# A down-projection whose range of row pairs moves by one per output pair, with results added to the residual in memory by DMA

## The chip, the cores and the metric

The kernel runs on one core of a Trainium2 chip. The metric is device time in microseconds: the median of several runs. A profile of one execution shows each engine: TensorE (PE, its weight loads apart as PEld), VectorE (DVE), ScalarE (ACT), GpSimd (POOL) and SyncE (SP), and the DMA queues.

## The reference, cut to what matters

One layer for 592 tokens (16 meta tokens, 512 of a prompt, 8 x 8 samples), model width 2048, all in fp32. After a mixer (recurrent and convolution heads) whose result is added to x, comes the part that the change touches:

```python
xn2 = rmsnorm(x, g_ffn)
up = jnp.einsum("btd,df->btf", xn2, w_up)          # 2048 -> 2 x 6144
gate, val = jnp.split(up, [D_FF], axis=-1)
gate_c, new_fconv = causal_dwconv(gate, st_fconv, conv_f_w)   # width 3
hid = jax.nn.gelu(gate_c + conv_f_b) * val
x = x + jnp.einsum("btf,fd->btd", hid, w_down)     # 6144 -> 2048
```

and then a final RMSNorm of x.

## The kernel before

Tokens lie along the free axis, features on the 128 partitions: 16 blocks of model rows, 48 of hidden rows. Each fp32 matmul is three fp32r ones (`hi*hi`, `hi*lo`, `lo*hi`): ACT rounds to the high part (`wh`, `fh`), DVE subtracts it for the low part (`wl`, `fl`).

The FFN (function `ffn`) multiplies pairs of blocks by halves of the tokens (290 wide in the up-projection, `H1`; 288 in the down-projection, `H2`) by the Strassen-Winograd scheme: 7 products instead of 8 (`PROD`, into four PSUM tiles, `BANKS`). For it, weights are summed on DVE (`raw`) and so are the right-hand sides (`forms`: `xt`, `fh`, `fl`, 7 forms of a row pair, which sit in one of 8 slots `h0..h7`, `l0..l7`). A *unit* is one row pair times one output pair: 7 products of 3 matmuls. A *group* of weights (`FG`, made by `ffn_groups`) is two units: SP loads 512 KB into one of two `raw` tiles, and `prep` makes `wh` and `wl`, 1792 wide, in two buffers each (`w_p`). `weights(q)` calls it one group ahead.

- Start: when the mixer ends, ACT and DVE split x1 into 16 `ph`/`pl`, POOL sums the squares and stores x1 into `xd`. Plain groups (`p`) go first; the norm stands behind the second of them. `build_x` then makes the 8 row pairs' forms in the slots.
- Up-projection: for each pair of hidden blocks a gate job (`done_f`: `combine`, `conv`, gelu) and a value job (`done_v`, which stores the hidden pair into `hd`).
- Down-projection: 22 row pairs, cut by `DSUB` into passes of 8, 8 and 6. Each pass goes through all 8 output pairs (job `("d", s, p)`). `build_h` loads a row pair from `hd` on POOL's queue and makes its forms; the next pass's are called during the last output pair of the pass before (or the last value job). `load_xp` loads the residual of an output pair, `done_d` adds the four PSUM tiles to it in seven operations on DVE, and, in the first two passes, stores it into `xe`.
- Tail (`t`): four hidden blocks that are left go through plain matmuls (`kh`, `kl`), `done_t` adds them to `xp`, and the final norm follows.

The order on each engine is set by a scheduler from the order of the code and its priorities (`urgent`, `high_priority`); a tile waits for the reader of its buffer's last use, and each engine runs its queue in order. `done_d` before:

Of the kernel before, what the change touches and what calls it, by code (L numbers as in the profile page):

```python
# [7 lines left out]
F32 = mybir.dt.float32  # L8
# [46 lines left out]
DSUB = (8, 8, 6)  # L55
NPL = 4
NTL = 4
SLOT = 8192
# [101 lines left out]
def ffn_groups():  # L160

    gs = []
    for r in range(NPL // 2):
        cols = [(0, 1), (NF, NF + 1)][r]
        for k0 in range(0, KD, 4):
            gs.append(("p", r, k0, [("w_up", k, c) for k in range(k0, k0 + 4) for c in cols]))

    def quad(src, f1, f2, kps):  # L170
        kk = [(k, c) for k, c in ((1, f2), (0, f1), (1, f1), (0, f2))]
        return [(src, 2 * kp + k, c) for k, c in kk for kp in kps]

    for m in range(NPL // 4, NF // 2):
        for o in (0, NF):
            for g in range(KD // 4):
                gs.append(("s", ("f" if o == 0 else "v", m), g, quad("w_up", o + 2 * m, o + 2 * m + 1,
                                                                 (2 * g, 2 * g + 1))))
    k0 = 0
    for s, n in enumerate(DSUB):  # L180
        for p in range(KD // 2):
            for g in range(n // 2):
# [12 lines left out]
PROD = {"P1": (0, 0), "P2": (1, 1), "R7": (2, 4), "R4": (3, 6), "Q3": (4, 2), "P6": (5, 5),  # L195
        "P5": (6, 3)}
BANKS = (("P6",), ("P2", "Q3"), ("P1", "R7"), ("P5", "R4"))
SBT = {"c": ("sb",), 0: ("sb", "o"), 1: ("sb", "z", "ev"), 2: ("sb", "z", "ev")}
X1T = ("fb", "v", "o", "z", "ev", "st", "sb", "xt")


def ffn(ctx, tc, xstack, one, dram, x1, rstd, ones, epst, warm, cv, wf, sfc, out, fst):

# [28 lines left out]
    w_p = pool("fw", 2)  # L232
# [6 lines left out]
    QP = MP - H1  # L239
# [3 lines left out]
    state = {"raw": 0, "spl": 0}  # L243

# [7 lines left out]
    def prep():  # L252
        q = state["spl"]
        while state["raw"] < min(q + 2, len(FG)):
            load()
        t = raws.pop(q)
        kind, _, i, _ = FG[q]
        if kind == "s":
            r = t.rearrange("p (s c) f -> p s (c f)", s=8)
            tt(r[:, 4:6], r[:, 2:4], r[:, 0:1].to_broadcast([P, 2, 2 * P]), AD)  # L260
            tt(r[:, 6], r[:, 5], r[:, 2], AD)
            tt(r[:, 7], r[:, 6], r[:, 1], AD)
            hi = w_p.tile([P, 7, 2 * P], F32R, tag="wh", name="wh")
            lo = w_p.tile([P, 7, 2 * P], F32R, tag="wl", name="wl")
            act(hi, r[:, 1:8], AF.Copy)
            tt(lo, r[:, 1:8], hi.bitcast(F32), SU)
        else:
            if kind == "p":
                hi = w_p.tile([P, 8, P], F32R, tag="wh", name="wh")
                lo = w_p.tile([P, 8, P], F32R, tag="wl", name="wl")  # L270
            else:
                j, o = divmod(i // 2, 2)
                if o == 0:
                    tail["h", j] = sl.tile([P, 16, P], F32R, tag=f"h{j}", name="th")
                    tail["l", j] = sl.tile([P, 16, P], F32R, tag=f"l{j}", name="tl")
                hi, lo = (tail[c, j][:, 8 * o:8 * o + 8] for c in "hl")
            act(hi, t[:, 0:8], AF.Copy)
            tt(lo, t[:, 0:8], hi.bitcast(F32), SU)
        spls[q] = (hi, lo)
        state["spl"] += 1  # L280

    tail = {}

    def weights(q, ahead=1):
        with tc.high_priority(offset=100):
            while state["spl"] <= min(q + ahead, len(FG) - 1):
                prep()
# [914 lines left out]
```

## Time and profile before

| what | us |
|---|---|
| median of 3 runs | 2752.55 (2749.21 to 2754.59) |
| the profiled execution's own time | 2755.04 |
| its span | 2753.3 |
| PE busy | 2621.3 |
| DVE busy | 1995.5 |
| ACT busy | 1127.9 |
| POOL busy | 506.4 |

All durations come from that one profiled execution, 2.5 us above the median. Its mean granted clock was 0.979 of full speed. By time, the mixer takes the span to 933 us, the up-projection goes to about 2060, the down-projection to about 2670, and the tail to the end. A stretch is read by its length against the number of matmuls that ran in it; in the waits of an engine, a row names who was waited for, how long in all, how often and how long at most. A PSUM tile is called `sgl` or `dbl`.

### The profile page before, as it was taken

What the parts mean: (1) busy time and instruction counts of PE and PEld (TensorE: products, weight loads), DVE (VectorE), ACT (ScalarE), POOL (GpSimd) and SP (SyncE); (2) the same over time, 40 slices, a digit from 0 to 9 for tenths busy, and PEclk for the clock granted to TensorE, in tenths of its full rate; (3) what the DMA queues carried; (4) which work ended last, traced back from release to release, by engine and by line L of the source; (5) the groups of instructions that cost most, each with busy time, mean ns of one, the idle gap of its engine ahead of it and who ended that gap; (6) DMA issues with size and microseconds to landing.
All of it is one profiled execution on the core that took longest, in us unless ns stands there. A gap on an engine that the chain in (4) does not pass through costs nothing. (4 is left out here: it accounts for less than half of the span.)

```text
span 2753.3 us, 45507 instructions
## 1 busy us (share of the span) xinstructions
PE 2621.3 (95%) x18974; PEld 2584.0 (94%) x18974; DVE 1995.5 (72%) x2534; ACT 1127.9 (41%) x1428; POOL 506.4 (18%) x665
## 2 busy tenths in 40 slices
PE   8999999999999989999999999999996997997987
PEld 8999999999999979999999999999996997997977
DVE  8663556546457598787878777878778779778776
ACT  5543434244234445444444444444444224223233
POOL 3341323223233511010101010101002002001002
PEclk9999999999999989999999999999998999998998
DMA  4222222222223333333333333333335444444232
GB/s 163 76 89 80 77 85 77 85 77 85 82 67 123 125 122 104 108 101 109 102 107 103 105 99 110 101 107 104 102 101 181 142 143 158 147 152 162 87 119 81
DMA packets 85406, 299.38 MB, mean 109 GB/s; under 512 B 10128, under 2 KB 14352, under 8 KB 85200
## 3 DMA queue, kind: packets, MB, share of 16 engines
q1 hardware_dynamic: 68720, 233.47, 27.5%
q0 software_dynamic: 16048, 62.55, 6.5%
q8 instruction: 149, 2.44, 0.4%
q14 instruction: 57, 0.47, 0.1%
q10 hardware_dynamic: 432, 0.46, 0.1%
HBM read 262.63 MB, written 33.80 MB: 108 GB/s over the span
## 5 line engine op out<-in xcount | busy, mean ns | idle before, releaser
L543 PE MATMUL dbl<-fh,wh 128*128 128x290 f32 (+1 forms) x3264 | 975.2, 299 | 20.6 <-DVE xp L211 15.7
L543 PE MATMUL dbl<-fl,wh 128*128 128x290 f32 (+1 forms) x3264 | 974.0, 299 | 1.3 <-DVE fl L211 1.3
L543 PE MATMUL dbl<-fh,wl 128*128 128x290 f32 (+1 forms) x3264 | 970.4, 299 | 3.0 <-DVE wl L211 3.0
L217 ACT ACTIVATE wh<-raw 128x1792 fp32r<-128x1792 f32 (+1 forms) x280 | 471.4, 1684 | 809.8 <-DVE raw L211 573.7
L211 DVE TENSOR_TENSOR wl<-raw,wh 128x1792 fp32r<-128x1792 f32 (+1 forms) x280 | 560.0, 2000 | 210.6 <-ACT wh L217 204.6
L543 PEld LDWEIGHTS dbl<-fh,wh 128*128 128x128 f32 x3264 | 623.2, 191 | 27.9 <-DVE xp L211 18.0
L543 PEld LDWEIGHTS dbl<-fh,wl 128*128 128x128 f32 x3264 | 623.5, 191 | 4.0 <-DVE wl L211 4.0
L543 PEld LDWEIGHTS dbl<-fl,wh 128*128 128x128 f32 x3264 | 623.7, 191 | 1.9 <-DVE fl L211 1.9
L211 DVE TENSOR_TENSOR raw<-raw 128x256 f32<-128x256 f32 (+1 forms) x816 | 416.0, 510 | 106.1 <-DMA raw<-wf 98.0
L1113 PE MATMUL ps<-xh,wl 128*128 128x290 f32 (+4 forms) x1536 | 336.8, 300 | 2.9 <-DVE wl L720 2.9
L1113 PE MATMUL ps<-xl,wh 128*128 128x290 f32 (+4 forms) x1536 | 335.1, 300 | 0.0
L732 ACT ACTIVATE wh<-raw 128x512 fp32r<-128x512 f32 x277 | 172.7, 628 | 395.5 <-PE ps L1113 341.1
L1113 PE MATMUL ps<-xh,wh 128*128 128x290 f32 (+4 forms) x1536 | 332.3, 298 | 2.3 <-ACT wh L732 1.7
L720 DVE TENSOR_TENSOR wl<-raw,wh 128x512 fp32r<-128x512 f32 x192 | 153.3, 804 | 193.6 <-ACT wh L732 193.3
L1113 PEld LDWEIGHTS ps<-xh,wl 128*128 128x128 f32 x1536 | 258.0, 191 | 3.1 <-DVE wl L720 3.1
L1113 PEld LDWEIGHTS ps<-xh,wh 128*128 128x128 f32 x1536 | 257.6, 191 | 3.3 <-ACT wh L732 1.9
L1113 PEld LDWEIGHTS ps<-xl,wh 128*128 128x128 f32 x1536 | 256.0, 190 | 0.0
L543 PE MATMUL sgl<-fh,wl 128*128 128x290 f32 (+1 forms) x544 | 172.7, 318 | 29.7 <-DVE wl L211 28.7
L543 PE MATMUL sgl<-fh,wh 128*128 128x290 f32 (+1 forms) x544 | 165.2, 304 | 37.7 <-ACT wh L217 34.2
L720 POOL TENSOR_TENSOR wl<-raw,wh 128x512 fp32r<-128x512 f32 x86 | 117.0, 1360 | 312.2 <-ACT wh L732 302.4
L543 PE MATMUL sgl<-fl,wh 128*128 128x290 f32 (+1 forms) x544 | 164.7, 303 | 2.9 <-DVE fl L211 2.9
L543 PEld LDWEIGHTS sgl<-fh,wl 128*128 128x128 f32 x544 | 104.7, 192 | 45.2 <-DVE wl L211 44.4
(214 smaller groups left out, 3291.0 us busy)
## 6 DMA issues: line engine op xcount, KB each, us to landing
raw<-wf SPq DMA_DIRECT2D x288, 512.0 KB, 3.6
raw<-w SPq DMA_DIRECT2D x135, 512.0 KB, 3.6
hd<-v POOLq DMA_DIRECT2D x24, 576.0 KB, 3.3
xe<-xp POOLq DMA_DIRECT2D x16, 576.0 KB, 3.8
xp<-xe POOLq DMA_DIRECT2D x16, 576.0 KB, 4.2
sb<-hd POOLq DMA_DIRECT2D x44, 144.0 KB, 2.5
sb<-hd POOLq DMA_DIRECT2D x22, 288.0 KB, 3.4
x<-x SPq DMA_DIRECT2D x16, 296.0 KB, 5.4
```

The source lines that it names most:

```text
L211: return (e or V).tensor_tensor(out=o, in0=a, in1=b, op=op)
L217: A.activation(out=o, in_=a, func=f, **k)
L543: mm = nc.tensor.matmul(o, l[a], r[z], start=i == 0 and u == 0 and k == 0, stop=i == n - 1 and u == 1 and k == 2)
L720: return (e or V).tensor_tensor(out=o, in0=a, in1=b, op=op)
L732: A.activation(out=o, in_=a, func=f, **k)
L1113: mm = nc.tensor.matmul(ps[:, b, 0:n], l, r[:, c0:c0 + n], start=(first and m == 0), stop=(last and m == 2))
```

## The change

It does five things. (1) The down-projection's passes are cut differently for each output pair (`CUT`), so that the range of row pairs moves by one from an output pair to the next: the first pass has 4, 5, 6, 7, 8, 8, 9, 9 units, the second 9 each, the third the rest (9 down to 4). There are nine slots (`NSL`), the ninth in buffers of the up-projection; `build_h` is called where `due` says: row pairs 0 to 3 in the last value job, 4 to 8 and 13 to 17 one at a time early in a job, 9 to 12 and 18 to 21 in four successive units of the last output pair of a pass. (2) `done_d` copies PSUM to tiles `e6`, `e23`, `e17`, `e54` on ACT, and five DMAs on POOL's queue add them to `xa` and `xb` in DRAM (in the first pass the two into `xb` write instead); `xa` gets the residual when the mixer ends, in 16 more stores. The tail loads `xa`, then adds `xb` into the tile by DMA. (3) Weights are split by half groups, 896 wide, in five buffers (`NWB`), prepared up to four halves ahead; their pool opens after x1's room is given back. (4) `combine`, `conv` and the hidden pair work on tiles in another layout: the convolution runs over 656 columns instead of 592, and the sample state comes by one small load per pair. (5) `kf`, `kh` and the tail's weights have rooms that come free earlier.

The diff, cut:

```diff
-DSUB = (8, 8, 6)
+CUT = [(0, a, a + 9, 22) for a in (4, 5, 6, 7, 8, 8, 9, 9)]
+NSL = 9
+NWB = 5
+TAILW = (4, 5, 0, 1)
...
-    w_p = pool("fw", 2)
...
     def prep():
-        q = state["spl"]
+        q, u = divmod(state["spl"], 2)
...
+            src, n = r[:, 1:8, u * P:u * P + P], 7
...
+            hi = w_p.tile([P, n, P], F32R, tag="wh", name="wh")
+            lo = w_p.tile([P, n, P], F32R, tag="wl", name="wl")
+            act(hi, src, AF.Copy)
+            tt(lo, src, hi.bitcast(F32), SU)
...
-    def weights(q, ahead=1):
+    def weights(q, ahead=NWB - 1):
...
-        nc.gpsimd.dma_start(out=xd[kp][:, o], in_=v)
+        nc.gpsimd.dma_start(out=xd[kp][:, 1 - o], in_=v)
+        nc.gpsimd.dma_start(out=xa[kp][:, 2 * o:2 * o + 2], in_=v[:, T1 - T0:])
     xstack.close()
+    w_p = pool("fw", NWB)
...
     def done_d(s, p, ps):
...
         with urgent():
-            tt(off, s6[:, 0:H2].unsqueeze(1).to_broadcast([P, 2, H2]), off, AD)
-            tt(on, w(dq), on, AD)
-            tt(t[:, 1], t[:, 1], dq[:, 1, 0:H2], SU)
-            tt(t[:, 2], t[:, 2], dq[:, 0, 0:H2], SU)
-            tt(on, w(dp), on, AD)
-            tt(off, w(dp), off, AD)
-            tt(off, w(dr), off, AD)
-        if s < len(DSUB) - 1:
-            xe[p] = dram.tile([P, 2, NTF], F32, name=f"xe{s}_{p}")
-            nc.gpsimd.dma_start(out=xe[p], in_=xp.pop(p))
+            act(e6, s6[:, 0:H2], AF.Copy)
+            act(e23[:, 0:4:3], w(dq), AF.Copy)
+            act(e23[:, 1], dq[:, 1, 0:H2], AF.Copy, scale=-1.0)
+            act(e23[:, 2], dq[:, 0, 0:H2], AF.Copy, scale=-1.0)
+            act(e17, w(dp), AF.Copy)
+            act(e54, w(dr), AF.Copy)
+        add = lambda o, i: nc.gpsimd.dma_start(out=o, in_=i, accum_op=AD)
+        add(xa[p][:, 1:3], e6.unsqueeze(1).to_broadcast([P, 2, H2]))
+        for i in range(2):
+            o, x = xb[p][:, 2 * i:2 * i + 2], e17[:, i:i + 1].to_broadcast([P, 2, H2])
+            if s:
+                add(o, x)
+            else:
+                nc.gpsimd.dma_start(out=o, in_=x)
+        add(xa[p], e23)
+        add(xb[p][:, 1:3], e54)
...
+    for k in range(CUT[0][3]):
+        u = (lastc, k) if k < 8 else lastu[k - NSL] if k >= NSL else (lastc, 7)
+        before = jobs[jobs.index(first[k]) - 1]
+        e = [j for j, kk in units].index(before)
+        due.setdefault(max(units.index(u), e if k > 3 else 0), []).append(k)
...
+    def load_xp(p, pl_, tag):
...
+        nc.gpsimd.dma_start(out=w, in_=xa[p])
+        nc.gpsimd.dma_start(out=w, in_=xb[p], accum_op=AD)
```

Where the instructions stand is shown at three places; a row has the line, the operation, the output and inputs with their buffers' numbers, and the shape. The first is ACT's queue where the mixer ends. Before, the first two weights of the FFN (`wh_9824`, `wh_9830`) stand among those of the mixer:

```order
L732 ACTIVATE sq_9021<-y_9017 128x580
L732 ACTIVATE sh_9022<-sq_9021 128x580
L732 ACTIVATE wh_9061<-raw_9059 128x512
L217 ACTIVATE wh_9824<-raw_9820 128x1024
L732 ACTIVATE wh_9093<-raw_9059 128x512
L217 ACTIVATE wh_9830<-raw_9822 128x1024
L732 ACTIVATE wh_9127<-raw_9125 128x512
L732 ACTIVATE wh_9159<-raw_9125 128x512
L732 ACTIVATE sq_9021<-aux_9177,epst_108 128x580
```

After, they (`wh_9858` and on) stand behind the last `ph` and the last square of x1 (`qa`):

```order
L215 ACTIVATE ph_9815<-x1_12_102,C_87 128x580
L215 ACTIVATE ph_9815<-x1_13_103,C_87 128x580
L215 ACTIVATE ph_9829<-x1_14_104,C_87 128x580
L215 ACTIVATE ph_9829<-x1_15_105,C_87 128x580
L215 ACTIVATE qa_9730<-x1_15_105 128x580
L215 ACTIVATE wh_9858<-raw_9854 128x512
L215 ACTIVATE wh_9862<-raw_9854 128x512
L215 ACTIVATE wh_9868<-raw_9856 128x512
L215 ACTIVATE wh_9872<-raw_9856 128x512
```

The first two groups of the FFN thereby moved behind the whole split of x1.

The second place is the end of an output pair of the first pass. Before, on DVE, the seven operations that add PSUM to `xp` stand between the weights' `raw` and `wl`:

```order
L211 TENSOR_TENSOR xp_22120<-sgl_22116,xp_22120 128x576
L211 TENSOR_TENSOR raw_22266<-raw_22266 128x512
L211 TENSOR_TENSOR wl_22272<-raw_22215,wh_22271 128x1792
L211 TENSOR_TENSOR raw_22266<-raw_22266 128x256
L211 TENSOR_TENSOR xp_22120<-dbl_22117,xp_22120 128x2x288
L211 TENSOR_TENSOR raw_22266<-raw_22266 128x256
L211 TENSOR_TENSOR xp_22120<-xp_22120,dbl_22117 128x288 x2
L211 TENSOR_TENSOR xp_22120<-dbl_22118,xp_22120 128x2x288
L211 TENSOR_TENSOR xp_22120<-dbl_22118,xp_22120 128x576
L211 TENSOR_TENSOR wl_22332<-raw_22266,wh_22331 128x1792
L211 TENSOR_TENSOR raw_22326<-raw_22326 128x512
L211 TENSOR_TENSOR xp_22120<-dbl_22119,xp_22120 128x576
```

After, on ACT, copies to the e tiles stand among the halves' `wh`:

```order
L215 ACTIVATE wh_23319<-raw_23213 128x896
L215 ACTIVATE e6_23353<-sgl_23108 128x288
L215 ACTIVATE e23_23354<-dbl_23109 128x2x288
L215 ACTIVATE e23_23354<-dbl_23109 128x288
L215 ACTIVATE wh_23328<-raw_23268 128x896
L215 ACTIVATE wh_23405<-raw_23268 128x896
L215 ACTIVATE e23_23354<-dbl_23109 128x288
L215 ACTIVATE e17_23355<-dbl_23110 128x576
L215 ACTIVATE e54_23356<-dbl_23111 128x576
```

and on POOL the DMAs that add them, with two row pairs' loads (`sb`) behind:

```order
L485 DMA xb5_9703<-e17_23082 128x2x288 x2
L478 DMA xb5_9703<-e54_23083 128x576
L478 DMA xa6_9696<-e6_23353 128x2x288
L478 DMA xa6_9696<-e23_23354 128x1152
L485 DMA xb6_9704<-e17_23355 128x2x288 x2
L478 DMA xb6_9704<-e54_23356 128x576
L372 DMA sb_23460<-hd10_9716 128x1152
L372 DMA sb_23472<-hd11_9717 128x1152
L478 DMA xa7_9697<-e6_23661 128x2x288
L372 DMA sb_23539<-hd12_9718 128x1152
```

The additions moved from DVE's queue to ACT's (copies) and POOL's (DMAs).

The third place is DVE's queue at the builds of a pass's row pairs. Before, during the last output pair of the first pass, where eight row pairs are built one after the other:

```order
L211 TENSOR_TENSOR fl_22830<-sb_22821,fh_22829 128x864
L211 TENSOR_TENSOR raw_22849<-raw_22849 128x512
L211 TENSOR_TENSOR wl_22855<-raw_22764,wh_22854 128x1792
L211 TENSOR_TENSOR raw_22849<-raw_22849 128x256
L211 TENSOR_TENSOR fl_22830<-xt_22825,fh_22829 128x1152
L211 TENSOR_TENSOR raw_22849<-raw_22849 128x256
L211 TENSOR_TENSOR xt_22839<-sb_22835 128x576
L211 TENSOR_TENSOR fl_22844<-sb_22835,fh_22843 128x864
L211 TENSOR_TENSOR xt_22839<-sb_22835,xt_22839 128x288
L211 TENSOR_TENSOR wl_22934<-raw_22849,wh_22933 128x1792
L211 TENSOR_TENSOR xt_22839<-sb_22835,xt_22839 128x288
L211 TENSOR_TENSOR raw_22928<-raw_22928 128x512
```

After, in the second pass's first output pair, where one row pair (`xt_23737`, `fl_23742`) is built:

```order
L209 TENSOR_TENSOR wl_23757<-raw_23680,wh_23756 128x896
L209 TENSOR_TENSOR wl_23803<-raw_23680,wh_23802 128x896
L209 TENSOR_TENSOR raw_23751<-raw_23751 128x256
L209 TENSOR_TENSOR fl_23742<-sb_23735,fh_23741 128x864
L209 TENSOR_TENSOR fl_23742<-xt_23737,fh_23741 128x1152
L209 TENSOR_TENSOR wl_23812<-raw_23751,wh_23811 128x896
L209 TENSOR_TENSOR wl_23858<-raw_23751,wh_23857 128x896
L209 TENSOR_TENSOR raw_23806<-raw_23806 128x512
L209 TENSOR_TENSOR xt_23988<-sb_23986 128x576
```

The rest of one build, and the start of the next (`xt_23988`), stand among the halves' weights; before, the builds of two row pairs (`fl_22830`, `xt_22839`) are mixed with those of one and a half groups, and six more builds follow in the same way.

More of the change, by code (lines that the diff above doesn't have):

```diff
@@ L292, in ffn @@
+    xb = [dram.tile([P, 4, H2], F32, name=f"xb{p}") for p in range(KD // 2)]
     hd = [dram.tile([P, 2, NTF], F32, name=f"hd{m}") for m in range(NF // 2)]
@@ L495, in ffn @@
-    ps = None
+    units = [u for g in FG if g[0] == "s" for u in g[1]]
+    left = {}
+    for j, k in units:
+        left[j] = left.get(j, 0) + 1
+    total = dict(left)
+    lastc = ("v", NF // 2 - 1)
+    lastu = {}
+    for j, k in units:
+        if j[0] == "d":
+            lastu[k] = (j, k)
+    jobs = list(dict.fromkeys(j for j, _ in units))
+    first = {}
+    for j, k in units:
+        if j[0] == "d":
+            first.setdefault(k, j)
+    due = {}
+    for k in range(CUT[0][3]):
[3 more added lines that the diff above has]
+        due.setdefault(max(units.index(u), e if k > 3 else 0), []).append(k)
@@ new lines, in ffn, with products @@
+    nunit = 0
+    ps = None
+    xp = {}
+    def load_xp(p, pl_, tag):
+        xp[p] = pl_.tile([P, 2, NTF], F32, tag=tag, name="xp")
+        w = xp[p].rearrange("p f (h m) -> p (f h) m", h=2)
+        nc.gpsimd.dma_start(out=w, in_=xa[p])
+        nc.gpsimd.dma_start(out=w, in_=xb[p], accum_op=AD)
+    def products(u, hi, lo, names, ps, H):
+        nonlocal mm
+        job, k = u
+        b, c, nm = names
+        o = ps[b][:, 0:H] if b == 0 else ps[b][:, c, 0:H]
+        wi, xi = PROD[nm]
+        l = hi[:, wi], lo[:, wi]
+        r = fx[k][0][xi], fx[k][1][xi]
+        for n, (a, z) in enumerate(((0, 0), (0, 1), (1, 0))):
+            mm = nc.tensor.matmul(o, l[a], r[z], start=left[job] == total[job] and n == 0,
+                                  stop=left[job] == 1 and n == 2)
@@ new lines, in ffn @@
+            H = H2 if i[0][0][0] == "d" else H1
+            for us in ([i] if same else [[i[0]], [i[1]]]):
+                job = us[0][0]
+                if job not in pst:
+                    pst[job] = (pss(), psd(), psd(), psd())
+                hold = left[job]
+                for n in NAMES:
+                    left[job] = hold
+                    for u in us:
+                        products(u, *halves[i.index(u)], n, pst[job], H)
+                        left[job] -= 1
+                if left[job] == 0:
+                    {"f": done_f, "v": done_v, "d": done_d}[job[0]](*job[1:], pst.pop(job))
+                    if job == lastc:
+                        nc.gpsimd.dma_start(out=fst.rearrange("p (n c) -> p n c", c=18), in_=fa)
+                for u in us:
+                    for k in due.get(nunit, ()):
+                        build_h(k)
+                    nunit += 1
+                if job == ("d", 2, 5) and left[job] == 0:
+                    for p, tag in enumerate(("o", "fb", "v")):
+                        load_xp(p, rp, tag)
@@ L1157 @@
     WF = np.zeros((len(FG), P, 8, P), np.float32)
-    for q, (_, _, _, tiles) in enumerate(FG):
+    for q, (_, _, tiles) in enumerate(FG):
         for o, (n, a, b) in enumerate(tiles):
```

380 lines of the change are left out of this document (171 added, 209 removed).

## The prediction

> **What bounds the kernel now.** I read the busy shares first, then the span cut into stages, then the waits of the matmul engine inside them, then the costs of single groups of instructions. The page says that TensorE is busy 95% of the span:
>
> ```profile
> span 2753.3 us, 45507 instructions
> ...
> PE 2621.3 (95%) x18974; PEld 2584.0 (94%) x18974; DVE 1995.5 (72%) x2534; ACT 1127.9 (41%) x1428; POOL 506.4 (18%) x665
> ```
>
> The change keeps the number of matmuls, so it can win only the stretches in which PE doesn't run at its rate. The next view has, for each stretch, its length, then busy time (and instructions) of PE, weight load, DVE, ACT, POOL, then the granted clock, the DMA share and GB/s:
>
> ```profile
> 200.00:600.00 400.00, 400.00 (x2962) 400.00 (x2961) 203.34 (x243) 142.51 (x206) 106.58 (x126) 1.00 0.27 81
> ...
> 930.00:1040.00 110.00, 92.24 (x601) 88.53 (x600) 101.02 (x143) 53.32 (x63) 25.10 (x33) 0.89 0.38 124
> 1040.00:2060.00 1020.00, 1003.32 (x7391) 992.52 (x7390) 805.39 (x1016) 463.65 (x616) 93.14 (x154) 1.00 0.33 104
> 2060.00:2140.00 80.00, 57.47 (x335) 52.92 (x335) 69.25 (x92) 36.33 (x38) 23.16 (x39) 0.85 0.51 163
> 2140.00:2300.00 160.00, 155.63 (x1161) 153.92 (x1160) 124.19 (x161) 49.89 (x32) 11.85 (x20) 1.00 0.46 148
> 2300.00:2350.00 50.00, 34.08 (x199) 30.39 (x198) 46.10 (x63) 20.23 (x16) 10.75 (x20) 0.83 0.47 148
> 2350.00:2500.00 150.00, 147.04 (x1098) 145.51 (x1097) 117.28 (x153) 48.27 (x31) 9.63 (x18) 1.00 0.46 153
> 2500.00:2550.00 50.00, 36.51 (x226) 33.88 (x225) 44.12 (x60) 16.18 (x13) 6.42 (x12) 0.83 0.48 154
> 2550.00:2670.00 120.00, 113.86 (x830) 110.56 (x830) 90.32 (x120) 33.53 (x21) 0.00 (x0) 1.00 0.29 90
> 2670.00:2690.00 20.00, 12.52 (x63) 11.54 (x62) 12.09 (x13) 9.59 (x11) 1.06 (x2) 0.74 0.50 175
> ```
>
> The first row is the yardstick: 2962 matmuls in 400 us, 0.135 us each. A stretch's length less its count times 0.135 is what it loses: 22 us in the up-projection (1040 to 2060), 34.8 at the start of the down-projection (2060 to 2140), 23.1 and 19.5 at its two pass changes (2300, 2500), 11.5 at the tail's start (2670), and 3, 2 and 8 in the three steady stretches between. There DVE is nearly full at the changes (69 of 80, 46 of 50, 44 of 50 us) and has a fifth of its time free elsewhere; the clock falls to 0.83 to 0.85 in them, so part of each loss is matmuls that run slowly after a pause. Who is late, from 2050 to 2690 and, last row, from 1060 to 2050 (total us, times, longest):
>
> ```profile
> PE sgl L543 <- ACT wh L217: 24.2, 9, 4.2
> PE dbl L543 <- DVE xp L211: 15.7, 25, 1.9
> PE sgl L543 <- DVE wl L211: 11.4, 11, 2.0
> PE dbl L657 <- ACT kh L217: 7.2, 2, 5.6
> ...
> PE sgl L543 <- DVE wl L211: 15.8, 36, 1.8
> ```
>
> Weights come late (DVE is building row pairs), PSUM is freed late by the residual adds (xp), and the tail waits for kh.
>
> **The change part by part.** The durations, from 2080 to 2680 (count, then busy us and mean ns), with the convolution's and one PSUM copy's rows of the up-projection last:
>
> ```profile
> L211 DVE TENSOR_TENSOR wl<-raw,wh 128x1792 fp32r<-128x1792 f32 x88 | 178.0, 2022 | 44.6 <-ACT wh L217 44.3
> ...
> L211 DVE TENSOR_TENSOR raw<-raw 128x256 f32<-128x256 f32 x174 | 73.4, 422 | 2.4
> L211 DVE TENSOR_TENSOR xp<-dbl,xp 128x576 f32<-128x576 f32 x96 | 71.3, 753 | 2.7 <-issue 1.8 <-PE dbl L543 0.7
> L211 DVE TENSOR_TENSOR raw<-raw 128x512 f32<-128x512 f32 x87 | 60.1, 691 | 54.8 <-DMA raw<-wf 54.5
> ...
> L211 DVE TENSOR_TENSOR fl<-xt,fh 128x1152 fp32r<-128x1152 f32 x21 | 28.4, 1354 | 0.4 <-ACT fh L217 0.4
> L217 ACT ACTIVATE fh<-xt 128x1152 fp32r<-128x1152 f32 x21 | 24.3, 1157 | 23.5 <-DVE xt L211 23.5
> L211 DVE TENSOR_TENSOR fl<-sb,fh 128x864 fp32r<-128x864 f32 x20 | 21.1, 1057 | 6.0 <-ACT fh L217 5.9
> L211 DVE TENSOR_TENSOR xp<-xp,dbl 128x288 f32<-128x288 f32 x48 | 20.3, 450 | 0.0
> L211 DVE TENSOR_TENSOR xt<-sb,xt 128x288 f32<-128x288 f32 x41 | 18.6, 455 | 0.1
> L211 DVE TENSOR_TENSOR xp<-sgl,xp 128x576 f32<-128x576 f32 x24 | 18.1, 756 | 6.2 <-PE sgl L543 6.0
> L217 ACT ACTIVATE fh<-sb 128x864 fp32r<-128x864 f32 x19 | 17.6, 924 | 48.5 <-DMA sb<-hd 38.9 <-PE dbl L543 9.3
> L211 DVE TENSOR_TENSOR xt<-sb 128x576 f32<-128x576 f32 x20 | 15.1, 755 | 0.0
> ...
> L214 DVE SCALAR_TENSOR_TENSOR fo<-fb,C,fo 128x592 f32<-128x592 f32 x80 | 64.7, 828 | 0.7
> ...
> L217 ACT ACTIVATE ev<-dbl 128x290 f32<-128x290 f32 x164 | 53.8, 421 | 0.5 <-PE dbl L543 0.5
> ```
>
> *Units of work.* A unit (a row pair for one output pair) is 21 matmuls, 21 x 0.135 = 2.8 us; a group of weights is two, 5.7 us, and costs DVE 0.69 + 2 x 0.42 + 2.02 = 3.55 us. Building a row pair's forms costs DVE 0.755 + 2 x 0.455 + 1.06 + 1.35 = 4.08 us. The add of an output pair costs it five 576-wide and two 288-wide operations, 5 x 0.755 + 2 x 0.45 = 4.7 us.
>
> *Weights in halves.* From the 864- and 1152-wide rows (1.03 ns a column on DVE, 0.81 on ACT) a half of 896 columns is estimated at 1.09 on DVE, 0.95 on ACT; a group then costs DVE 3.71, 0.16 more. A half is ready one half sooner, and five of them run two and a half groups ahead instead of two. That is more than the longest wait (1.8 us) in the up-projection, so its 36 waits should go, and with them most of the 22 us. Against it: per pair of gate and value jobs (8 groups, 45 us) 8 x 0.16 = 1.3 us, and the convolution's four operations 64 columns wider, 4 x 0.07, 1.5 in all; over 22.7 pairs 34 us of DVE time, in a stretch with 215 us free. I take -18; the ends are -22, all of the loss gone, and +12, all 34 uncovered.
>
> *Builds spread.* Before, the next pass's 8 or 6 builds fall into the last output pair of a pass; 8 x 4.08 = 33 us of DVE work on top of 14 us for its own weights meets 23 us of matmuls. After, four are at the start of the down-projection, one at most job starts, and two bursts of four at the passes' ends, each called 14 units (40 us) ahead of its first use. A burst then asks 4 x 3.71 + 4 x 4.08 = 31 us of DVE in four groups of 23 us: 8 us late, of which two groups of prepared weights (up to 5.7 us of lead) cover over half. I leave 4 lost at each change: -35 of 42.6 (ends 0 and -43). At the start, DVE still has the last value job's work and four builds ahead of short first jobs; I leave 10 of 34.8 lost: -25 (ends 0 and -35).
>
> *The add leaves DVE.* 4.7 us per output pair go from DVE. ACT gets six copies out of PSUM: three of 288 at 0.42, three of 576 estimated at 0.65 (0.42 + 288 x 0.81 ns), 3.2 us, and is busy 49.9 of 160 us there. They stand in ACT's queue among the weights' wh, so a copy whose e tile hasn't left yet holds up wh behind it. PSUM should come free sooner: the 15.7 us of xp waits go, but part of them is in the stretches counted above. I take -8 of the steady stretches' 13 (ends -13 and +5, a copy's wait of 0.2 us at each of 24 jobs).
>
> *Five DMAs that add.* No transfer here adds on its way, so the nearest rows are plain ones (KB each, us to landing):
>
> ```profile
> xe<-xp POOLq DMA_DIRECT2D x16, 576.0 KB, 3.8
> xp<-xe POOLq DMA_DIRECT2D x16, 576.0 KB, 4.2
> ...
> sb<-hd POOLq DMA_DIRECT2D x22, 288.0 KB, 3.4
> ```
>
> Per output pair the DMAs carry 12 blocks of 147 KB, 1.77 MB, and the xe stores and loads go. Without those, weights (512 KB per 5.7 us) and one build per job (0.59 MB per 20.5 us) are some 123 GB/s, a share of 0.38 by the 0.46 at 148 GB/s. The adds are 1.77 MB per 20.5 us, 86 GB/s: 0.27 if a byte costs as much as in a plain transfer, 0.54 at double, 0.80 at triple. Added to 0.38: 0.65, 0.92, 1.18. The jobs of 4 units (three, 11.2 us) and 5 (three, 14 us) come to 0.87 and 0.77 at one, 1.36 and 1.16 at two: (0.36 x 11.2 + 0.16 x 14) x 3 = 19 us over. At one nothing is over; at three all is, 0.18 x 492 us = 89. An add reads its target as well as writing it, so I take double: +18, between 0 and +89. The Trainium skill, "Collectives: The Full Stack", Stop ④ (SDMA + CCE), has the add done in the DMA's own path in one memory pass, read, read and write; three moves to a plain transfer's two would be 1.5 times, 4 us by the same working, and the sum 14 lower. No row here shows it, and the 2 to 4 KB pieces here are smaller than xe's, so double stands.
>
> *Mixer to FFN.* The weights' pool now opens only after x1's room is given back, so the first two weights stand behind the 16 ph and pl, which start when the mixer ends, in order of time and, last, what one store of x1 takes on POOL:
>
> ```profile
> 934.80 7.47 ACT L217 ACTIVATE ph<-x,C 128x580 fp32r<-128x580 f32 x11
> ...
> 944.85 3.45 ACT L217 ACTIVATE ph<-x,C 128x580 fp32r<-128x580 f32 x5
> ...
> 935.65 10.87 DVE L214 SCALAR_TENSOR_TENSOR pl<-x,C,ph 128x580 fp32r<-128x580 f32 x11 [1.85 <-ACT ph L217]
> ...
> 947.58 3.75 DVE L214 SCALAR_TENSOR_TENSOR pl<-x,C,ph 128x580 fp32r<-128x580 f32 x5
> ...
> 935.61 1.12 PE L515 MATMUL dbl<-ph,wh 128*128 128x290 f32 x4 [2.62 <-ACT ph L217]
> ...
> L310 POOL DMA_DIRECT2D xd<-x x5 | 2.8, 561 | 0.0
> ```
>
> Before, PE starts at 935.6; after, wl of the first half comes at 935.65 + 10.87 + 3.75 + about 0.7 = 951. That is up to 15 us, less what PE waited for pl in its first groups; the next work after the norm is bound by DVE, which in the gap does what it would have done later, and four products per build become two (8 x 0.3 us saved). I take +9 (ends 0 and +16). Sixteen more stores into xa at 0.56 us of POOL each stand ahead of the xr loads; 9 us; these are read only after the norm, which comes behind two groups of 48 matmuls (13 us), so they cost nothing unless that cover goes.
>
> *Tail.* kf and its split come before the last jobs end and the tail's weights are split ahead: 11.5 less about 2.5 for the last adds, -9 (ends -11 and +5: the residual now has to land, then be loaded and summed).
>
> Sum: -18 - 25 - 35 - 8 + 18 + 9 - 9 = -68, so 2687 against the profiled execution's own 2755.0 us; that one lies 2.5 over the median of 2752.55, so **2685**.
>
> **The rivals.** (1) *The adds bind at the short jobs.* The e tiles have one buffer each. On POOL e23's add waits for e6's to land, e54's for e17's; behind them in that queue stand the next sb loads. Three landings of 3.4 to 4.2 us are 11 us, as long as a job of 4 units, and late e tiles hold up ACT, so wh. The rule behind the waits is in the Trainium skill, "DMA: Bandwidth & Descriptors", Rules for kernel authors: an accumulating DMA must wait for an earlier one on the same bytes. At 2.5 times a plain byte the excess is 25 us by the mean, 46 job by job (20, 15, 7 and 4 in jobs of 4, 5, 6 and 7 units): 2755 - 86 + 46 - 2.5 = 2712. For it: DMA is 0.46 busy already; against: latency is hidden while a job takes 20 us. Case 2705 to 2750.
> (2) *Slower: the adds bind throughout.* From about three times a plain byte (0.38 + 0.80 over 1) the DMA engines set the pace of all 492 us: 2755 - 86 + 89 - 2.5 = 2755, no gain; each half more costs 0.13 x 492 = 66, so 2821 at 3.5. For it: 2.3 KB rows and an unknown read of the target; against: the plain rows land 576 KB in 3.8 us, 150 GB/s from one transfer alone.
> (3) *The builds bunch all the same.* DVE takes its queue in order; if builds and weights still come together at the changes, T's -35 becomes -10 and the start's -25 becomes -10: 2725, inside (1).
> (4) *No change*, if (1) and the mixer's end together take what is won.
>
> **How the numbers follow.** Forecast 0.62 (own range 2655 to 2705: adds at one, 2666, to two with 4 at the mixer's end and the bursts 16 worse); rivals (1) and (3) 0.20; slower 0.10; no change 0.04, within 0.2% or 5.5 us, about what this kernel's three runs (5.4 us apart) can tell; below 2655, all terms at their good ends, 0.04. So faster 0.86, same 0.04, slower 0.10. The range 2652 to 2750 leaves out slower, no change and a part of the last.
>
> **What would show it.** In the profile after: no xp waits, and ACT copies near 3.2 us a job; in the up-projection few waits for wl; the pass changes with clock near 1.00 and under 5 us lost; 10 to 16 us of PE idle near 935 to 951; DMA share in the down-projection near 0.9 (0.65 would put adds at the price of plain bytes, 1.00 would prove rival 1 or 2), and landings of the adds near 4 us. I am wrong if ACT waits for DMA in the short jobs, or if PE waits for fl at the changes.

## The result, and the profile after

The changed kernel takes 2885.14 us (median of 4 runs, 2876.33 to 2889.07) against 2751.36 before: 1.048 times as long, 95% interval 1.045 to 1.051. The forecast was 2685 with a range of 2652 to 2750. Its profiled execution took 2876.33 us, 121 more than the one before; the sums below go against that. It was the fastest of its four, 9 us under their median, so differences of stages come out smaller than differences of medians.

The page after says that TensorE is busy for longer with as many matmuls:

```profile
span 2874.5 us, 46494 instructions
...
PE 2659.9 (93%) x18974; PEld 2609.3 (91%) x18974; DVE 1939.1 (67%) x2651; ACT 1209.0 (42%) x1784; POOL 563.2 (20%) x708
```

Cut by stages (mixer's last matmul, first one of the up-projection, of the down-projection, of the tail, the tail's last one), with the columns of the stretches shown before. The kernel before, then the changed one:

```profile
933.00:994.00 61.00, 56.29 (x387) 55.20 (x388) 54.31 (x73) 31.12 (x39) 15.70 (x21) 0.94 0.42 137
994.00:2086.00 1092.00, 1059.06 (x7734) 1045.01 (x7734) 875.70 (x1116) 500.76 (x657) 108.83 (x177) 0.99 0.34 106
2086.00:2677.00 591.00, 523.38 (x3695) 506.61 (x3693) 471.54 (x621) 191.13 (x132) 53.68 (x97) 0.95 0.44 141
2677.00:2737.00 60.00, 56.93 (x391) 55.41 (x392) 39.97 (x66) 27.28 (x52) 14.46 (x16) 0.92 0.24 81
```

```profile
933.00:1008.00 75.00, 55.95 (x394) 55.14 (x393) 57.89 (x77) 36.88 (x54) 23.87 (x26) 0.86 0.41 137
1008.00:2104.00 1096.00, 1065.18 (x7730) 1041.13 (x7729) 901.44 (x1306) 507.82 (x771) 59.87 (x143) 0.99 0.34 105
2104.00:2785.00 681.00, 554.80 (x3699) 534.70 (x3697) 392.03 (x547) 262.96 (x365) 135.57 (x145) 0.89 0.69 155
2785.00:2860.00 75.00, 61.29 (x398) 59.33 (x398) 35.96 (x64) 27.50 (x54) 25.68 (x31) 0.87 0.64 157
```

The last window before ends 1.8 us short of its last matmul; up to that one the tail takes 61 to 62 us. By stage the 121 us are +14 between mixer and up-projection, +4 in the up-projection, +90 in the down-projection and +13 in the tail. In the down-projection VectorE has 79 us less to do than before and stands idle more. What TensorE waits for there, and what VectorE waits for (total us, times, longest), after:

```profile
PE dbl L533 <- ACT e L215: 45.7, 20, 16.5
PE sgl L533 <- DVE wl L209: 39.7, 29, 7.3
PE sgl L533 <- ACT wh L215: 22.0, 13, 6.9
PE dbl L699 <- ACT e L215: 13.8, 1, 13.8
```

```profile
DVE raw L209 <- DMA raw<-wf: 114.9, 60, 4.2
DVE xt L209 <- DMA sb<-hd: 65.0, 15, 13.0
```

Before, from the first matmul of the stage to the first of the tail, the same rows of the weights and of raw were:

```profile
PE sgl L543 <- ACT wh L217: 22.1, 8, 4.2
PE sgl L543 <- DVE wl L211: 10.4, 10, 2.0
DVE raw L211 <- DMA raw<-wf: 54.5, 45, 2.4
```

The waits for xp (15.7 us) went, and waits for the e copies, three times as long, came. Weights come late for 62 us instead of 33. VectorE waits for transfers twice as long for raw weights, and for the row pairs, which weren't in its list before. The DMAs of the stage after (KB each, median us to landing) are:

```profile
raw<-wf SPq DMA_DIRECT2D x90, 512.0 KB, 4.5
xb<-e POOLq DMA_DIRECT2D x69, 288.0 KB, 5.3
xa<-e POOLq DMA_DIRECT2D x23, 576.0 KB, 7.0
sb<-hd POOLq DMA_DIRECT2D x19, 576.0 KB, 5.6
xa<-e POOLq DMA_DIRECT2D x24, 288.0 KB, 4.9
```

Before, the loads of weights landed in 3.6 us.

One output pair (1,3) shows how it comes about. First GpSimd's queue, then VectorE's and TensorE's (start, us, what, and in brackets the idle time before it and what ended it):

```profile
2416.03 1.20 POOL L478 DMA_DIRECT2D xa<-e  x1 [12.50 <-ACT e L215]
2421.52 0.90 POOL L478 DMA_DIRECT2D xa<-e  x1 [4.29 <-ACT e L215]
2422.14 1.53 POOL L478 DMA_DIRECT2D xb<-e  x1
2430.73 1.19 POOL L478 DMA_DIRECT2D xb<-e  x1 [7.07 <-DMA xb<-e]
2436.08 0.88 POOL L478 DMA_DIRECT2D xb<-e  x1 [4.16 <-issue]
2436.63 0.89 POOL L372 DMA_DIRECT2D sb<-hd  x1
```

```profile
2433.80 1.09 DVE L209 TENSOR_TENSOR wl<-raw,wh 128x896 fp32r<-128x896 f32 x1 [0.15 <-ACT wh L215]
2442.83 0.76 DVE L209 TENSOR_TENSOR xt<-sb 128x576 f32<-128x576 f32 x1 [7.93 <-DMA sb<-hd]
```

```profile
2446.68 0.61 PE L533 MATMUL sgl<-fh,wl 128*128 128x288 f32 x1 [4.64 <-DVE wl L209]
```

The five adds take 20 us from the first issue (2416.0) to the last (2436.1), where I had counted 11. So it is in the second and third pass (19 to 22 us); in the first, where two of the five are plain writes, it is 12 to 17. The row pair's load stands behind them and lands 6 us later. VectorE meets that row pair's first operation at 2434.9 and stands there for 7.9 us, with the weights' sums behind it in its queue; TensorE then waits 4.6 us for a wl.

The largest single losses are at the end. TensorE waits 16.5 us for an e copy in the last output pair (at 2759) and 13.8 us at the tail's first matmul; ACT, which makes these copies, waited there 15.2 and 13.5 us for adds into xa to land. By the time of each output pair less its units x 2.805 us (21 matmuls of 0.1336 us), the last output pair loses 32.7 us.

### The profile page after: what moved, and what is told of

Read it like the earlier page. It is cut to its first block, busy times and chain, and to the rows that moved or that the text cites. A ratio compares the mean times of both kernels' runs of the same rounds, so it can differ in the third digit from the quotient of the medians.

```text
span 2874.5 us, 46494 instructions
## 1 busy us (share of the span) xinstructions
PE 2659.9 (93%) x18974; PEld 2609.3 (91%) x18974; DVE 1939.1 (67%) x2651; ACT 1209.0 (42%) x1784; POOL 563.2 (20%) x708
## 5 line engine op out<-in xcount | busy, mean ns | idle before, releaser
L533 PE MATMUL dbl<-fh,wh 128*128 128x290 f32 (+1 forms) x3264 | 997.2, 306 | 68.8 <-ACT e L215 45.7
L533 PE MATMUL dbl<-fh,wl 128*128 128x290 f32 (+1 forms) x3264 | 982.2, 301 | 0.3 <-DVE wl L209 0.3
L215 ACT ACTIVATE wh<-raw 128x896 fp32r<-128x896 f32 (+1 forms) x560 | 519.6, 942 | 857.0 <-DVE raw L209 659.6
L209 DVE TENSOR_TENSOR wl<-raw,wh 128x896 fp32r<-128x896 f32 (+1 forms) x560 | 597.6, 1076 | 206.0 <-ACT wh L215 203.3
L533 PEld LDWEIGHTS dbl<-fh,wh 128*128 128x128 f32 x3264 | 633.4, 194 | 95.3 <-ACT e L215 51.1
L533 PEld LDWEIGHTS dbl<-fl,wh 128*128 128x128 f32 x3264 | 634.4, 194 | 4.7 <-DVE fl L209 4.7
L533 PEld LDWEIGHTS dbl<-fh,wl 128*128 128x128 f32 x3264 | 633.9, 194 | 0.6 <-DVE wl L209 0.6
```

The costliest lines, as they stand in the source:

```text
L209: return (e or V).tensor_tensor(out=o, in0=a, in1=b, op=op)
L215: A.activation(out=o, in_=a, func=f, **k)
L533: mm = nc.tensor.matmul(o, l[a], r[z], start=left[job] == total[job] and n == 0, stop=left[job] == 1 and n == 2)
```

## The experiments

All are timed against the kernel before, which was run again with each group of them; its medians there were 2745.4 to 2748.9 us, and a ratio goes by the one beside it. Stage lengths are from each run's own profile: from the mixer's last matmul to the next one (gap), from the first matmul of the up-projection to the first of the down-projection (up), and so on; "down" is the down-projection.

| run | median us | ratio to before, 95% | gap | up | down | tail |
|---|---|---|---|---|---|---|
| before | 2751.4 | | 3.0 | 1091 | 592 | 61 |
| changed | 2885.1 | 1.048 (1.045, 1.051) | 16.8 | 1096 | 681 | 75 |
| x1 loads of row pairs on SyncE | 2835.4 | 1.032 (1.030, 1.033) | 16.8 | 1096 | 642 | 74 |
| x2 plain writes | 2765.2 | 1.006 (1.005, 1.008) | 16.8 | 1094 | 575 | 66 |
| x3 one add | 2746.1 | 0.999 (0.998, 1.000) | 16.7 | 1098 | 569 | 61 |
| x4 one sum, three adds | 2829.1 | 1.029 (1.028, 1.031) | 16.8 | 1093 | 645 | 67 |
| x5 x4, loads on SyncE | 2831.2 | 1.031 (1.029, 1.033) | 16.8 | 1098 | 647 | 67 |
| x6 early weights, four halves | 2810.5 | 1.023 (1.022, 1.025) | 5.6 | 1058 | 652 | 86 |
| x7 before, half weights | 2694.6 | 0.982 (0.980, 0.983) | 3.0 | 1054 | 570 | 59 |
| x8 combined | 2678.0 | 0.975 (0.973, 0.977) | 5.6 | 1059 | 543 | 60 |
| x9 three halves ahead | 2835.6 | 1.032 (1.030, 1.035) | 16.8 | 1074 | 660 | 72 |
| x10 x4, four halves | 2763.4 | 1.006 (1.004, 1.008) | 5.7 | 1057 | 630 | 61 |
| x11 x10, three raw buffers | 2739.6 | 0.997 (0.996, 0.998) | 16.8 | 1057 | 596 | 57 |
| x12 x6, two e buffers | 2809.3 | 1.022 (1.020, 1.025) | 5.7 | 1059 | 645 | 89 |
| x13 x6, three raw buffers | 2787.7 | 1.015 (1.013, 1.017) | 5.6 | 1057 | 633 | 81 |
| x14 x13, loads on SyncE | 2736.3 | 0.995 (0.993, 0.996) | 5.6 | 1056 | 586 | 82 |
| x15 combined, three raw buffers | 2661.2 | 0.968 (0.966, 0.970) | 5.6 | 1056 | 533 | 57 |

**x1: the loads of row pairs off the adds' queue.**

```diff
-        nc.gpsimd.dma_start(out=sb, in_=hd[kp]...
+        nc.sync.dma_start(out=sb, in_=hd[kp]...
```

> The changed kernel with one edit: the loads of row pairs (hd to sb) are issued on SyncE's queue instead of GpSimd's, so they no longer stand behind the adding DMAs and their waits. Theory Q (the adds are a chain of about 20 us per output pair on GpSimd's queue, the next row pair's load stands behind it, VectorE then stands at that row pair's build, and weights come late behind it): VectorE's waits for sb in the down-projection fall from 65 us to under 20, TensorE's waits for wl and wh there from 62 us to about 30, the time to about 2845 us; TensorE's wait for the e copies (46 us) stays. Theory B (the adds' bytes fill the DMA engines, and everything is late by that): the loads are as late as before, time within 10 us of 2885.

The median fell by 50 us; the profiled executions differ by 39, and all of it is in the down-projection. VectorE's wait for sb there is now

```profile
DVE xt L209 <- DMA sb<-hd: 12.3, 7, 4.4
```

and TensorE's for wl and wh 40.7 us; its wait for the e copies stays, at 47.3. So the place of these loads behind the chain costs some 40 us. It leaves 50 us of the stage's loss against before. The last output pair still loses 32.4 us.

**x2: the adds as plain writes.**

```diff
-        add = lambda o, i: nc.gpsimd.dma_start(out=o, in_=i, accum_op=AD)
+        add = lambda o, i: nc.gpsimd.dma_start(out=o, in_=i)
```

> The changed kernel with the adding DMAs of an output pair made plain writes (the sums are left out: later ones overwrite earlier ones), same bytes from the same tiles, same order and same waits. It prices an add against a write. If an add costs a DMA engine about double, the DMA share of the down-projection falls from about 0.67 to about 0.5, landings of the 576 KB ones from 7.0 us to about 4. Both theories then expect less time: Q because four landings in a row get shorter, about 2840 us; B because the load falls, about 2790.

This run leaves the sums out. The time fell by 120 us, more than either theory expected, so it doesn't tell them apart: the chain got shorter too (12.8 us from first to last issue, median, instead of 20), and the last output pair loses 7.9 us. The down-projection is 575 us and the 576 KB DMAs into xa landed in 4.0 us instead of 7.0. The share of 16 DMA engines that GpSimd's queue (q0) and the weights' queue (q1) took in the down-projection (packets, MB, share), in the changed kernel (682 us), in x2 (575 us) and in x3 (569 us):

```profile
q0 software_dynamic: 26387, 57.24, 46.2%
q1 hardware_dynamic: 13104, 47.72, 22.3%
```

```profile
q0 software_dynamic: 14640, 56.93, 29.0%
q1 hardware_dynamic: 12884, 46.95, 26.0%
```

```profile
q1 hardware_dynamic: 12956, 47.18, 27.0%
q0 software_dynamic: 6928, 28.31, 22.3%
```

For GpSimd's queue that is 315, 167 and 127 us of all engines. Plain bytes go at 57 MB in 167 us, 342 MB per ms. In the changed kernel 36.3 of the 57.2 MB are adds (24 x 0.295 + 23 x 0.59 + 53 x 0.295); the other 20.9 take 61 us, so the adds take 254 where plain bytes would take 106: 2.4 times. In x3, 13.6 MB of adds take 84 us for 40: 2.1 times. The weights' packets cost 3.2 to 3.3 us of all engines per MB in all three, so a packet's time isn't longer for crowding. Part of the 2.4 may be smaller packets, since GpSimd's queue had 26387 of them in the changed kernel and 14640 in x2 for the same MB; x3's packets are as large as x2's (4 KB), and there it is 2.1. The price I took, double, was about right. What an add costs beyond that isn't in its engines' time.

**x3: one sum on VectorE, one add.**

```diff
-            act(e6, ...); act(e23, ...) x3; act(e17, ...); act(e54, ...)
-        add(xa[p][:, 1:3], e6...); add or write (xb[p]..., e17...) x2; add(xa[p], e23); add(xb[p][:, 1:3], e54)
+        t = rp.tile([P, 4, H2], F32, tag=("e23", "ea")[(s * 8 + p) % 2], name="et")
+            act(off, s6[:, 0:H2].unsqueeze(1).to_broadcast([P, 2, H2]), AF.Copy)
+            act(on, w(dq), AF.Copy)
+            tt(t[:, 1], t[:, 1], dq[:, 1, 0:H2], SU)
+            tt(t[:, 2], t[:, 2], dq[:, 0, 0:H2], SU)
+            tt(on, w(dp), on, AD); tt(off, w(dp), off, AD); tt(off, w(dr), off, AD)
+        nc.gpsimd.dma_start(out=xa[p], in_=t, accum_op=AD)
```

> The changed kernel, but an output pair's four PSUM tiles are summed into one tile (two ACT copies, five VectorE operations), in two buffers by turns, and one DMA of 576 KB adds it to xa; xb goes. A third of the adds' bytes, one landing instead of a chain. Both theories expect the down-projection to fall from 681 us to about 560 and the tail's start to lose under 8 us; time about 2765 us, since 13 us at the mixer's end stay.

The down-projection is 569 us and the tail 61: of the 139 us that this wins on the changed kernel, 112 and 14 are there. By output pair (its length less units x 2.805 us), the steady ones now lose about 1 us each, but the first loses 10.9, the third 11.5, the two that follow a burst of four builds 13.4 and 13.0, and the last one 6.9.

**x4 and x5: as many bytes, no chain.** Two more adds of the same tile go to scratch (plain writes there in the first pass); in x5 the row pairs' loads are on SyncE.

```diff
+        for x in (xb[p], xc[p]):
+            nc.gpsimd.dma_start(out=x, in_=t, accum_op=AD)   # a plain write where s == 0
```

> As the run with one add, but the same tile is added to three tensors in memory by three DMAs that don't wait for one another (two of them to scratch that nothing reads, written plainly in the first pass): as many bytes as in the changed kernel, no chain. Q: within 15 us of the run with one add (about 2775). B: near the changed kernel, 2850 or more.

> The run with one sum and three adds (2829 us), with the loads of row pairs issued on SyncE's queue. Theory P: what the adds cost is mostly the place of these loads, behind the adds' data in GpSimd's queue (one took 10 us there, with VectorE standing 7 us at the build); then this run falls to 2785 or less, within 40 us of the run with one add (2746). Theory L: the adds' load on the DMA engines itself (about double a plain byte) makes the weights' loads late too; then it stays at 2810 or more.

x4 lies between the two theories, nearer to B: 83 us over x3, 56 below the changed kernel. x5 changes nothing (2831 us), so without the chain the loads' place costs nothing, and theory P falls. But the DMA engines are only 0.59 busy in x4's down-projection:

```profile
2101.00:2746.00 645.00, 536.25 (x3696) 520.63 (x3695) 451.00 (x666) 232.09 (x272) 69.92 (x95) 0.92 0.59 158
```

```profile
DVE raw L209 <- DMA raw<-wf: 100.6, 35, 7.8
```

```profile
PE dbl L528 <- DVE et L209: 70.5, 28, 6.1
```

The three adds are issued together and land after 5.6, 8.4 and 11.0 us (medians). Loads of weights fall among them: 24 of the 90 took over 6 us, in x3 two. Over the 24 output pairs VectorE stands 11 times at such a load for 4 to 8 us, 65 of its 100.6 us (in x3 never for more than 4), and behind it in its queue stand the operations that free PSUM. That made a third theory: what counts is how late a single load is, against how early it was asked for.

**x10 and x11: a load asked for earlier.**

```diff
-NWB = 5
+NWB = 4
-    raw_p = pool("fraw", 2)          # x11 only, and three loads ahead instead of two
+    raw_p = pool("fraw", 3)
```

> The run with one sum and three adds, with four halves of weights instead of five: the base of the next run. Up-projection about 1058 instead of 1093, down-projection within 15 us of 645, time about 2790.

> The same with three raw buffers instead of two, so that a weights' load is issued a group (5.7 us) earlier. In the run with three adds VectorE stood 4 to 8 us, about once per output pair, at a weights' load that fell into the adds' 11 us, and behind it in its queue stood the operations that free PSUM. Theory burst (average load isn't the limit, a load's lateness is): VectorE's waits for raw in the down-projection fall from about 100 us to under 40, the down-projection by 30 us or more. Theory throughput (the DMA engines can't carry adds and weights): no change within 10 us.

With a third raw buffer the down-projection falls by 34 us, to 596, with the same three adds. VectorE still stands at raw for 91.5 us (110.8 in x10), so that part of the expectation was wrong. But it gets there earlier: its first operation on a group starts 13.5 us (median) ahead of the group's first matmul, 8.6 in x10, since the load was issued 19.8 us ahead instead of 14.3. TensorE's wait for the copies, 38.2 us in x10, is

```profile
PE dbl L528 <- DVE et L209: 14.1, 10, 4.0
```

The theory of throughput falls. x10 also says that four halves remove 11 us of the gap, 36 us of the up-projection and 15 us of the down-projection; 2790 us were expected of it, 2763 came.

**x6, x9: how many halves, and how far ahead.**

```diff
-NWB = 5                                   # x6: 4, and its pool opened with the raw buffers
-    def weights(q, ahead=NWB - 1):        # x9: five buffers, three halves ahead
+    def weights(q, ahead=3):
```

> The changed kernel with the weights' pool opened before x1's room is given back, which takes four halves instead of five. The first two groups can again be split before the mixer ends: from the mixer's last matmul to the first plain one 3 us instead of 16.8, the time 10 to 14 us less, about 2873. If the fifth half were worth something in the up-projection, that stage would grow from 1096 us by some us.

> The changed kernel with weights prepared three halves ahead instead of four (all five buffers stay, the pool opens as late as in the changed kernel). In the run with early weights the up-projection fell from 1096 to 1058 us, and this tells whether the number ahead or the pool's place did it. If the number ahead (a fourth half's wl stands in VectorE's queue ahead of the operations that free PSUM): up-projection near 1058, the wait at the mixer's end stays 16.8, time about 2835 to 2850. If the place: up-projection 1096, time 2885.

x6 won 75 us where 12 were expected, 38 of them in the up-projection and 29 in the down-projection; its tail is 11 us longer. x9 came out in time as expected, but its up-projection lies between the two cases. 1000 us of that stage in the changed kernel, in x9 and in x10, then what TensorE waited for there in the changed kernel:

```profile
1054.00:2054.00 1000.00, 984.19 (x7207) 965.65 (x7206) 816.77 (x1184) 465.46 (x714) 51.37 (x129) 1.00 0.34 105
```

```profile
1054.00:2054.00 1000.00, 987.99 (x7340) 981.98 (x7340) 836.18 (x1209) 475.49 (x719) 59.44 (x131) 1.00 0.34 107
```

```profile
1044.00:2044.00 1000.00, 999.24 (x7484) 998.84 (x7483) 845.06 (x1231) 476.52 (x741) 67.15 (x134) 1.00 0.35 109
```

```profile
PE dbl L533 <- DVE v L209: 4.2, 13, 0.8
PE dbl L533 <- DVE fb L209: 2.8, 6, 0.8
PE dbl L533 <- ACT v L215: 1.6, 2, 1.0
```

7207, 7340 and 7484 matmuls: with four buffers TensorE runs without a pause, 0.1336 us each. Five buffers and four halves ahead bring waits for the operations that free PSUM. The rows above add up to 9 us of idle time; counted from start to start, 164 matmuls of the changed kernel come more than 0.2 us after the one before and lose 37 us, 25 of them the first into a PSUM tile that a v or fb operation has just freed and 9 the ones right behind. Three ahead take away more than half of the loss (22 of 38 us by the stage's length). That the fourth half's wl stands ahead of those operations in VectorE's queue fits this, and wasn't shown apart. Why five buffers at three ahead still lose 17 us stays open; there too it is mostly at PSUM that v operations free (14 of 20 us in the 1000).

The gap is the fifth half's too. In x10 the pool is opened where the changed kernel opens it, after x1's room is given back, and the gap is 5.7; in x11, which uses more room, it is 16.8 again. So it isn't the place in the code. It fits that a pool that takes room of x1 waits for x1's last readers, but no run shows that wait by itself.

**x7: half weights alone, on the kernel before.** Groups of two units as before, split by halves into four buffers, three halves ahead; passes, adds on VectorE and `xe` stay.

> The kernel before with one part of the change alone: weights split by halves, in four buffers (the room of the two whole ones), three halves ahead. If the 36 waits for wl in the up-projection (21 us of lost matmul time) go and nothing takes their place, the up-projection falls from 1091 us to about 1072 and the time to about 2730. If the time of PSUM's release binds next, as it does in the changed kernel, it gains under 5 us.

51 us faster than the kernel before beside it, where some 20 were expected; by the profiles 38 in the up-projection and 22 in the down-projection, where the three starts of a pass still lose 23.2, 18.2 and 12.0 us. With part (4) of the change, the other layout of the convolution, four halves come to 1058 us in the up-projection (x6), without it to 1054 here, so that part costs about 4 us there.

**x12 to x14: the two causes in the changed kernel itself.** All with four halves, as x6. x12 has two buffers for e23, e17 and e54; x13 a third raw buffer, in room that x1 gives back; x14 that and the row pairs' loads on SyncE.

> The run with early weights (2810 us; the changed kernel's five adds per output pair) with two buffers for e23, e17 and e54 instead of one. ACT's waits for the adds' landings (64 us in the down-projection there) and TensorE's for ACT's e copies (41.5 in it, 10.6 at the tail) come from the single buffers, if theory Q's chain matters on that side too: both fall by more than half, the time to about 2780. If the copies only wait because everything is late, it stays within 10 us of 2810.

> The run with early weights (2810 us, the five adds of the changed kernel) with a third raw buffer. If late weights' loads are what the adds cost in the changed kernel too, the down-projection falls from 652 us by 25 or more, as it did by 34 in the run with three adds. If there the row pairs' loads, behind the chain of adds on GpSimd's queue, hold VectorE, it falls by less than 10: about 2805 us.

> The same, with the row pairs' loads on SyncE's queue too. Both causes taken away: the down-projection should be near that of the run with three adds and three raw buffers (596 us) plus what ACT and the tail wait for the chain (30 to 40 us): 620 to 635, time about 2775 us. If the loads' place counts only where the raw buffers are two, it stays with the run before it.

x12's time is that of x6, but not because nothing changed. ACT's waits for landings at e23, e17 and e54, 61 us in x6 (down-projection and tail), went; 37 us came at e6, which kept its one buffer, and TensorE's wait for the e copies in the down-projection fell from 41.5 to 22.7 us, while at the tail its waits for the last copies and sums grew from 29 to 44. So the single buffers do hold ACT; what doubling all four would win wasn't run. x13 won 19 us in the down-projection, between the two expectations, and x14 another 47, more than expected. With all five adds, the stage is then

```profile
2056.00:2642.00 586.00, 523.17 (x3702) 510.92 (x3700) 387.21 (x548) 262.78 (x362) 121.88 (x123) 0.94 0.76 180
```

586 us at a DMA share of 0.76: less than before the change (591), with the same adds that took 681 (and four halves instead of five, worth 29 us there in x6). What doesn't go away is the end: the last output pair loses 28.3 us and the tail takes 82, since all adds of an output pair have to land before its sum is loaded, and the last jobs of 4 and 5 units (11 and 14 us) are shorter than the chain's 20 us.

**x8 and x15: combined.** x3's one add; four halves, their pool opened early; the row pairs' loads on SyncE; the builds of a burst two units apart; in the up-projection ACT copies the third PSUM tile's diagonal so that VectorE can add it later. x15 has a third raw buffer too.

```diff
-        due.setdefault(max(units.index(u), e if k > 3 else 0), []).append(k)
+        d = max(units.index(u), e if k > 3 else 0)
+        due.setdefault(d + {10: 2, 11: 4, 12: 6, 13: 3, 19: 2, 20: 4, 21: 6}.get(k, 0), []).append(k)
```

> The run with one add, with: weights' pool opened early (four halves), row pairs' loads on SyncE's queue, the bursts of four builds spaced two units apart, and in the up-projection the third PSUM tile's diagonal copied out by ACT so that VectorE adds it later. Expected from 2746: -12 at the mixer's end, -15 from the bursts (13 us lost at each), -10 from PSUM freed sooner in the up-projection, about 2709 us; at worst 2735, if only the first holds.

> The combined run (2678 us) with a third raw buffer in room that x1 gives back. VectorE still waits 34 us for raw there, and TensorE 13 us for weights and 19 for the PSUM copies: 5 to 12 us less, about 2669, if lateness of loads is still behind them; within 4 us of 2678 if it is VectorE's own work.

2678 and 2661 us, 31 and 8 less than expected; in x8 the up-projection gave 39 us where 10 were counted, about what four halves give alone (x6, x10). x15 is 0.968 of the kernel before (0.966 to 0.970). With the builds apart, the output pairs after a burst lose 2.2 and 2.9 us in x8 and 1.5 and 1.3 in x15, instead of 13.4 and 13.0 in x3. Other edits lie between them and x3, and the spacing wasn't tested alone; x14, which has five adds, keeps the bursts and shares the four halves, the third raw buffer and SyncE's loads with x15, loses 7.1 and 6.2.

## Why the prediction was wrong, step by step

- **Weights in halves, -18.** The stage came out 4 us longer. The effect was there and larger than forecast: halves alone win 38 us in the up-projection (x7). The loss was undercounted: the yardstick of 0.135 us comes from the mixer, and by the 0.1336 at which this stage can run (x10) it had lost 33 us, not 22. The step that failed is "five of them run two and a half groups ahead", counted as a gain alone: the fifth half costs 36 to 38 us there, 15 to 29 in the down-projection and 11 at the mixer's end (x6, x10), and 22 of the first come with the fourth half ahead (x9).
- **Builds spread, -35 and -25.** Right in kind. In x3 the steady output pairs lose 1 us, but a burst of four still costs 13 where 4 were left, and the start 22 where 10 were. My reading is that four builds called in four successive units fill VectorE's queue ahead of the weights, so that the 14 units of lead were of no use; two units apart, with other edits, they cost 1.3 to 2.9 (x8, x15). In x2, where VectorE has no sums, the same two output pairs lose 2.0 and 2.4, as forecast, though others there lose up to 7.
- **The add leaves VectorE, -8.** The xp waits went as forecast; 45.7 us of waits for ACT's e copies took their place, and 13.8 more at the tail's start. The two long ones, 16.5 and 13.8, are shown to be the chain's, since ACT waited 15.2 and 13.5 us for adds to land; the others are short (0.3 to 6.0 us), and what made ACT late there wasn't taken apart.
- **Five DMAs that add, +18.** This is the step that decided. The price of a byte (double) held: 2.1 to 2.4 times. What failed is how it was turned into time: the adds were spread evenly over each job and cost something only where the mean share passed 1. The stage lost its time at a mean share of 0.69, and runs in 586 us at 0.76 (x14). Against x3, which has one add, the adds cost 112 us in the down-projection and 14 in the tail, in three ways: weights' loads land late among the adds' data, more than two raw buffers cover (19 us in x13, 34 in x11); row pairs' loads wait behind the chain on GpSimd's queue (39 us in x1, 47 in x14); and the last output pair waits for the chain, 32.7 us against 6.9 in x3, which none of these edits takes away (28.3 in x14).
- **Mixer to FFN, +9.** 13.8 us, inside its bounds. The reason is the room that the buffers take, not where the pool is opened (x10, x11).
- **Tail, -9.** 13 us slower, beyond the bad end of +5. The waits for kh (7.2 us before) went as forecast; the sum that now has to land first was the mis-sized term: TensorE waits 13.5 us for xp, one time 9.0, behind the chain of the short last jobs. With one add the tail takes 61 us, as before.
- **The rivals.** The first had the mechanism, with its place on GpSimd's queue, the loads behind it and ACT held up; it was priced at 46 us, from engine time again and 11 us of chain where the trace has 20: the adds landed in 4.9 to 7.0 us (medians) where the plain rows had 3.4 to 4.2, and the second add of e17 waited for the first, which wasn't counted. The slower one had the sign and a time near the result (2821 at 3.5 times), by a cause that x11 and x14 rule out: the DMA engines' throughput. The third, that the builds bunch all the same, fits x3: 26 us left at the changes and 22 at the start, where it had 33 and 25. The chance of 0.10 for slower was too low because the first and the slower one were taken for one question, what a byte costs. The prediction's own sign of being wrong came true, ACT waiting for DMA in the short jobs; the other, waits for fl at the changes, didn't (1.5 us).

## What to carry to other kernels

Price a transfer by where it stands and when it comes, not by its share of the DMA engines: ask which load will land among a burst, how much earlier it was asked for, and what stands behind the instruction that waits for it in its engine's queue. DMAs that wait for one another belong on a queue where no load that feeds a critical engine stands behind them, and several adds to one target are better one. More buffers and a longer lead aren't free: they take room whose last user must be done, and they put work that isn't urgent ahead of work that is.

## What was new about the hardware

An adding DMA of fp32 from SBUF into memory, issued from GpSimd, took 2.1 to 2.4 times the engine time of a plain write, and 7.0 us instead of 4.0 to land 576 KB (changed kernel and x2). The Trainium skill, "Collectives: The Full Stack", Stop ④ (SDMA + CCE), has one pass of read, read and write with the add free. My estimate from it, three moves for a plain transfer's two, was 1.5; the trace shows more.

In the second and third pass the second of the two adds of e17 starts 0.3 us after the first has landed, in all 16 output pairs and in each of the runs with five adds (x1, x6, x9, x12 to x14), 5 to 13 us after the first's start. They write different halves of `xb`. The profile names the wait in two of the 16 of the changed kernel (one is the 7.07 <-DMA xb<-e above), and "issue" in the others. As plain writes (x2) the two go out 0.7 us apart in 15 of the 16, long before the first has landed, and x4's adds of a whole tile into three tensors 0.6 us apart. So adds into the same tensor went one after the other. Whether the order of the kernel or the chip asks for it isn't shown.
